# Moving weight tiles to other byte offsets, halving 512-column matmuls and turning query with value tiles in a fused HGRN2 and ConvFFN layer

## The chip, the cores and the metric

The kernel runs on one core of one Trainium2 chip. The metric is the device time of one execution in microseconds (us); the time of a kernel is the median of several executions. Five engines of the core work beside each other: PE (TensorE, the matmuls), DVE (VectorE), ACT (ScalarE), POOL (GpSimd) and SP (SyncE, which here issues the transfers).

## The reference

One layer over 256 latent and 256 context tokens with a model width of 2048: a bidirectional gated recurrence as token mixer, then a gated MLP with a width-3 convolution, each between two RMS norms with adaLN shift, scale and gate.

```python
q, f_fw, f_bw, v, g = jnp.split(h @ w_in, 5, axis=-1)          # w_in: 2048 x 10240
...
f = lb + (1 - lb) * jax.nn.sigmoid(f_raw)
dirs.append((heads(1 - f), heads(jnp.log(f))))
...
S = exp(b_end) * S + einsum('bhsk,bhsv->bhkv', kc * exp(b_end - b), vc)   # chunked scan, both directions
...
o = rms_norm(o, o_gain) ; y = (o * jax.nn.silu(g)) @ w_out     # 2048 x 2048
x_lat = x_lat + gt_ml * rms_norm(y, norm_mix_post)
...
gate, up = jnp.split(h @ ffn_w_in, 2, axis=-1)                 # 2048 x 11264
f = (silu(dwconv_centred(gate, conv_w, conv_b)) * up) @ ffn_w_out   # 5632 x 2048
x_lat = x_lat + gt_fl * rms_norm(f, norm_ffn_post)
```

Only the latent tokens leave the layer, so queries and gates are made for 256 tokens, and forget gates and values for all 512.

## The kernel before, in words

All large products are made in three float32r matmuls. `split` turns each float32 operand into a part `hi`, which ACT rounds to float32r, and the rest `lo`, which DVE subtracts; `mm3` (lines 197 to 202) then adds hi·hi, hi·lo and lo·hi into one PSUM bank. A matmul has a stationary operand, loaded into the array, and a moving operand that streams through it, one column after the other; the trace has a weight load (PEld) for each matmul.

A weight tile is 512 KB. The class `Stream` holds the list of all 452 weight tiles in the order of their use: `load` issues the DMA into one of four `w_raw` buffers, `prep` makes `w_hi` and `w_lo` (three buffers each, 4096 bytes per partition) a little ahead of the matmuls, and `next` hands a tile out. The order of the tiles is thus written by hand, in the calls of `ws.add`; the engines' own order follows from the code and the priorities in it, by a scheduler.

The stages in order of time are these.

- The start (to about 240 us): for each of eight pairs of row blocks the tokens are normed and modulated, and the first 512 columns of q, g, v and both forget gates are accumulated in SBUF (`start_latents`, `start_v`, `start_f`).
- The mixer's projections (240 to 890 us): for the head pairs p = 2 to 7, forget gates of both directions (`proj_ws` with 512 moving columns, tokens moving, weights stationary), queries (`one_bank`, `proj_ws` with 256 columns), values (`proj_xs`, weights moving, tokens stationary) and gates (`one_bank` again). After each tile `step` moves the generator `mixer` on, so that the scans of earlier head pairs (`scan`: strips of 32 columns, decays on DVE, copies on ACT, the readout `o`) lie between the projections' matmuls. `scan(p)` begins when the queries of p are there, and waits inside for v and g.
- The mixer's output product (890 to 985 us): `out_product` with z stationary and `w_out` moving, 512 columns; the rest of the last scan runs beside it (`mixed`, two steps for each weight tile).
- The norm between (985 to 1013 us).
- The MLP's first product (1013 to 1490 us): `ffn_w_in` stationary, h2 moving, 256 columns, with convolution and activation beside it.
- The MLP's output product (1490 us to the end): `out_product` with the activations `ah` and `al` stationary and `ffn_w_out` moving, 512 columns.

Where tiles lie in SBUF is set by their size and by tiles that hold nothing (`spacer`). Before the change the weights' parts start at 64 bytes modulo 256 in their partition, and the operands that meet them at 0:

```python
    SHIFT = 64
    edge = ctx.enter_context(tc.tile_pool(name="edge", bufs=1, side="right"))
    spacer(edge, 224)
...
        spacer(wpool, SHIFT)
...
        spacer(h2, 256 - SHIFT)
...
        spacer(hold[0], SHIFT)
```

Of the kernel before, what the change touches and what calls it, by code (L numbers as in the profile page):

```python
# [8 lines left out]
F32 = mybir.dt.float32  # L9
# [8 lines left out]
P = 128  # L18
# [18 lines left out]
def tile_hgrn2_convffn_layer(  # L37
# [26 lines left out]
    SHIFT = 64  # L64
# [43 lines left out]

    class Stream:
# [6 lines left out]
        def add(self, src, a, n):  # L116
            self.specs.append((src, a, n))

        def load(self, n):
            while len(self.raw) < min(n, len(self.specs)):  # L120
                src, a, w = self.specs[len(self.raw)]
# [7 lines left out]
        def prep(self, pool=wpool):  # L129
            i = len(self.done)  # L130
            with tc.high_priority(offset=0 if i < n_start else 400):
                self.load(i + 1)
                _, a, w = self.specs[i]
# [3 lines left out]
                hi = pool.tile([P, a, w], F32R, name="w_hi")  # L137
                lo = pool.tile([P, a, w], F32R, name="w_lo")
# [30 lines left out]
    for j2 in range(8):  # L169
        for sec in "qgvfb":  # L170
            ws.add(w_in[j2 * 256:(j2 + 1) * 256, SEC[sec]:SEC[sec] + 512].rearrange("(a p) n -> p a n", p=P), 2, 512)
    n_start = len(ws.specs)
    for p in range(2, NP):
        for sec in "fbqvg":
            for k4 in range(4):
                ws.add(in_src(sec, p, k4), 4, 256)
# [5 lines left out]
    def add_out(w, chunks):  # L182
        for c0, n in chunks:
            rows = P * (1024 // n)
            for r in range(0, w.shape[0], rows):
                ws.add(w[r:r + rows, c0:c0 + n].rearrange("(a p) n -> p a n", p=P), rows // P, n)

    add_out(w_out, MIX_CHUNKS)

    ws.plain = range(len(ws.specs), len(ws.specs) + PLAIN)  # L190
    for i in range(NFF):
        for up in range(2):
            for k4 in range(4):
                col = up * DFF + i * 256
                ws.add(ffn_w_in[k4 * 512:(k4 + 1) * 512, col:col + 256].rearrange("(a p) n -> p a n", p=P), 4, 256)
    add_out(ffn_w_out, FFN_CHUNKS)
# [12 lines left out]
    colsC = const.tile([P, P], F32, name="colsC")  # L209
    colsD = const.tile([P, P], F32, name="colsD")  # L210
# [313 lines left out]
    with tc.manual_schedule():  # L524
# [6 lines left out]
        spacer(wpool, SHIFT)  # L531
# [66 lines left out]
    def proj_ws(banks, wt, k4, width, first, last):  # L598
        hi, lo = wt
        for k in range(4):  # L600
            kt = k4 * 4 + k
            for h in range(2):
# [3 lines left out]
                    first and k == 0 and (own or h == 0), last and k == 3 and (own or h == 1))  # L606
# [275 lines left out]
    for p in range(2, NP):  # L882
# [46 lines left out]
    def mixed():  # L929
# [17 lines left out]
        spacer(h2, 256 - SHIFT)  # L947
# [10 lines left out]
        spacer(hold[0], SHIFT)  # L958
# [195 lines left out]
```

## Time and profile before

| | us |
|---|---|
| median of three runs | 1751.97 |
| the three runs | 1737.32, 1751.97, 1755.46 |
| the profiled execution, its own time | 1740.89 |
| its span, first to last instruction | 1738.9 |
| PE busy in the span | 1691.3 (97%) |
| DVE, ACT busy | 1154.2 (66%), 772.5 (44%) |

The profile is one execution. A matmul's entry lasts longer than its place in the stream, because the next one starts while it still drains; what the stream pays for one matmul is the distance between starts. It can be read from a stretch without gaps: a row of the view of stretches counts every matmul that touches the stretch, so the distance is (length of the stretch + mean duration of one) / count.

### The profile page before, as it was taken

The numbers are of one execution on the slowest core, as the hardware profiler recorded it, in microseconds if no ns is written. First come the engines' busy times: TensorE is split into PE (matmuls) and PEld (weight loads), VectorE is DVE, ScalarE is ACT, GpSimd is POOL, SyncE is SP. The second block draws the span as 40 slices with busy tenths as digits, with TensorE's granted clock in tenths as the row PEclk, the third lists the DMA queues.
The fourth block names the chain that finished last, engine by engine and source line by source line (L and its number), as shares of the span: only waits on it lengthen the run. The fifth ranks groups of instructions, "written<-read, shape, count | busy, mean of one in ns | idle before, by whom it ended". The sixth has DMA issues, their size and how long they took to land.

```text
span 1738.9 us, 31985 instructions
## 1 busy us (share of the span) xinstructions
PE 1691.3 (97%) x12990; PEld 1504.6 (87%) x12990; DVE 1154.2 (66%) x1856; ACT 772.5 (44%) x1176; POOL 3.4 (0%) x13
## 2 busy tenths in 40 slices
PE   6999999899999999999999899999999999999998
PEld 4777888888989889898988799999999999888886
DVE  5777798865548875588565688766666666544444
ACT  4322264454545344443454544444444444443443
POOL 0000000000000000000000000000000000000000
PEclk9999999999999999999999999999999999999999
DMA  9897657633326863677348579766666666655654
GB/s 349 284 294 240 224 172 233 209 110 110 109 74 199 280 224 99 194 234 246 115 154 277 183 243 324 250 194 194 192 193 194 194 194 194 203 196 193 200 192 147
DMA packets 274646, 352.57 MB, mean 203 GB/s; under 512 B 12954, under 2 KB 197675, under 8 KB 273987
## 3 DMA queue, kind: packets, MB, share of 16 engines
q1 hardware_dynamic: 274499, 350.53, 62.5%
q8 instruction: 102, 1.67, 0.4%
q14 instruction: 45, 0.37, 0.1%
HBM read 348.37 MB, written 2.11 MB: 202 GB/s over the span
## 4 chain that ended last, share of the span: by engine, by line
PE 81%; DVE 8%; DMA 6%; issue 2%; ACT 1%; SPq 0%; DVEq 0%; ACTq 0%
PE pj L200 25%; PE pj L202 25%; PE pj L201 25%; DMA ada_w<-in_ada_w_dram 4%; DVE ada_acc L363 3%; DVE w_lo L107 2%; PE o L416 1%; ACT w_hi L106 1%; DVE k L692 1%; PE mi L804 1%; PE sc L732 1%; DMA w_raw<-in_hgrn_w_in_dram 1%; DMA aw<-in_ada_w_dram 1%; DMA hTh<-in_x_dram 0%; PE o L823 0%
## 5 line engine op out<-in xcount | busy, mean ns | idle before, releaser
L107 DVE TENSOR_TENSOR w_lo<-w_raw,w_hi 128x1024 fp32r<-128x1024 f32 x452 | 552.5, 1223 | 396.3 <-ACT w_hi L106 392.7
L106 ACT CAST w_hi<-w_raw 128x1024 fp32r<-128x1024 f32 x452 | 472.9, 1048 | 683.3 <-PE pj L201 367.9
L202 PE MATMUL pj<-h2h,w_lo 128*128 128x256 f32 x1376 | 381.0, 277 | 3.9 <-DVE w_lo L107 3.9
L200 PE MATMUL pj<-h2h,w_hi 128*128 128x256 f32 x1376 | 380.3, 276 | 0.0
L201 PE MATMUL pj<-h2l,w_hi 128*128 128x256 f32 x1376 | 380.0, 276 | 0.0
L200 PE MATMUL pj<-hTh,w_hi 128*128 128x256 f32 (+1 forms) x1040 | 353.2, 340 | 3.5 <-ACT w_hi L106 1.9
L202 PE MATMUL pj<-hTh,w_lo 128*128 128x256 f32 (+1 forms) x1040 | 348.0, 335 | 0.7 <-DVE w_lo L107 0.6
L201 PE MATMUL pj<-hTl,w_hi 128*128 128x256 f32 (+1 forms) x1040 | 348.2, 335 | 0.0
L202 PEld LDWEIGHTS pj<-h2h,w_lo 128*128 128x128 f32 x1376 | 258.4, 188 | 5.6 <-DVE w_lo L107 5.5
L200 PEld LDWEIGHTS pj<-h2h,w_hi 128*128 128x128 f32 x1376 | 258.3, 188 | 0.9 <-issue 0.8
L201 PEld LDWEIGHTS pj<-h2l,w_hi 128*128 128x128 f32 x1376 | 258.4, 188 | 0.0
L200 PEld LDWEIGHTS pj<-hTh,w_hi 128*128 128x128 f32 x1040 | 196.3, 189 | 33.7 <-issue 5.0
L202 PEld LDWEIGHTS pj<-hTh,w_lo 128*128 128x128 f32 x1040 | 196.3, 189 | 24.6 <-DVE w_lo L107 1.1
L201 PEld LDWEIGHTS pj<-hTl,w_hi 128*128 128x128 f32 x1040 | 196.7, 189 | 21.6 <-DVE hTl L107 0.2
L363 DVE SCALAR_TENSOR_TENSOR ada_acc<-ada_w,cst,ada_acc 128x512 f32<-128x512 f32 x240 | 179.7, 749 | 45.3 <-DMA ada_w<-in_ada_w_dram 42.2
L202 PE MATMUL pj<-w_hi,al 128*128 128x512 f32 x352 | 138.7, 394 | 0.0
L201 PE MATMUL pj<-w_lo,ah 128*128 128x512 f32 x352 | 138.0, 392 | 0.0
L200 PE MATMUL pj<-w_hi,hTh 128*128 128x256 f32 (+1 forms) x448 | 136.1, 304 | 0.6 <-DVE q L468 0.6
L200 PE MATMUL pj<-w_hi,ah 128*128 128x512 f32 x352 | 136.6, 388 | 0.0
L202 PE MATMUL pj<-w_hi,hTl 128*128 128x256 f32 (+1 forms) x448 | 134.0, 299 | 0.0
L201 PE MATMUL pj<-w_lo,hTh 128*128 128x256 f32 (+1 forms) x448 | 133.8, 299 | 0.0
L200 PEld LDWEIGHTS pj<-w_hi,hTh 128*128 128x128 f32 x448 | 85.9, 192 | 4.8 <-DVE stage L466 1.1
(226 smaller groups left out, 1792.1 us busy)
## 6 DMA issues: line engine op xcount, KB each, us to landing
w_raw<-in_ffn_w_in_dram SPq DMA_DIRECT2D x172, 512.0 KB, 3.9
w_raw<-in_hgrn_w_in_dram SPq DMA_DIRECT2D x160, 512.0 KB, 4.2
ada_w<-in_ada_w_dram SPq DMA_DIRECT2D x256, 256.0 KB, 4.0
w_raw<-in_ffn_w_out_dram SPq DMA_DIRECT2D x88, 512.0 KB, 3.6
aw<-in_ada_w_dram SPq DMA_DIRECT2D x64, 512.0 KB, 8.7
w_raw<-in_hgrn_w_out_dram SPq DMA_DIRECT2D x32, 512.0 KB, 4.2
hTh<-in_x_dram SPq DMA_DIRECT2D x2, 1024.0 KB, 4.9
hTh<-in_ctx_dram SPq DMA_DIRECT2D x2, 1024.0 KB, 10.3
```

What stands on the lines that cost most here:

```text
L106: S.copy(out=hi, in_=src)
L107: V.tensor_tensor(out=lo, in0=src, in1=hi.bitcast(F32), op=ALU.subtract)
L200: PE.matmul(out=o, lhsT=lh, rhs=rh, start=first, stop=False, skip_group_check=True)
L201: PE.matmul(out=o, lhsT=lh, rhs=rl, start=False, stop=False, skip_group_check=True)
L202: PE.matmul(out=o, lhsT=ll, rhs=rh, start=False, stop=last, skip_group_check=True)
L363: V.scalar_tensor_tensor(out=acc, in0=aw, scalar=cst[:, r, 0:1], in1=acc, op0=ALU.mult, op1=ALU.add)
L416: PE.matmul(out=strip[32 * a:32 * (a + 1), :], lhsT=cst[:, r4 * 4 + a, :], rhs=aws[r4][:, a].rearrange("p s n -> p (s n)"), start=(r4 == 0 ...
L692: V.tensor_tensor(out=half(t, i, m), in0=half(t, i, m), in1=half(by, 1 - i, m)[:, :, 0:1].to_broadcast([P, 256 // m, m]), op=ALU.mult)
L732: PE.matmul(out=o[32 * b:32 * b + 32, 32 * i:32 * i + 32], lhsT=flat(lhs[b % 2])[:, s0:s0 + 32], rhs=flat(rhs[b % 2])[:, t0:t0 + 32], star ...
L804: PE.matmul(out=sps[:, cs], lhsT=kT[:, d, h, ct], rhs=v[:, 2 + ct, h * P:(h + 1) * P], start=(ct == 0), stop=(ct == 1))
```

## The change

It has three parts.

- Placement. Each weight part gets a tile of 4096 + 128 bytes, and its data start at a chosen byte of it: 76 where the weights are stationary (q, g, f, b, `ffn_w_in`, and all tiles of the start), 64 where they move (v, `w_out`, `ffn_w_out`). Since 4224 is 16 x 256 + 128, the three buffers start at 0, 128 and 0 modulo 256 by turns, so stationary weights lie at 76 or 204 and moving ones at 64 or 192; a spacer of 128 bytes makes `w_hi` and `w_lo` of one tile equal modulo 256. The spacers of before go; h2 now lies at 128 modulo 256, the tokens, z and the MLP's activations stay at 0. `colsC` and `colsD` are cut to 96 columns, which gives 256 bytes of room.
- Halves. `mm3` can make a 512-column product as two of 256 columns, the three matmuls of the first half and then those of the second. The forget gates (in the start for whole tiles, and in `proj_ws` where each head has its own bank) and the MLP's output product use it.
- In turn. For p = 2 to 7 a query tile and a value tile now alternate, four of each, with one `step` of 1.5 for a pair instead of 0.5 after each query tile and 1.0 after each value tile. The queries of p are complete only when its values are.

```diff
-    SHIFT = 64
+    STATIONARY, MOVING = 76, 64
...
+    def placed(pool, a, w, name, place):
+
+        t = pool.tile([P, a * w + 32], F32R, name=name)
+        return t[:, place // 4:place // 4 + a * w].rearrange("p (a n) -> p a n", a=a)
...
-                hi = pool.tile([P, a, w], F32R, name="w_hi")
-                lo = pool.tile([P, a, w], F32R, name="w_lo")
+                hi = placed(pool, a, w, "w_hi", place)
+                if i == 0:
+
+                    spacer(wpool, 128)
+                lo = placed(pool, a, w, "w_lo", place)
                 split(hi, lo, self.raw[i])
...
-        for sec in "fbqvg":
+        for secs in ("f", "b", "qv", "g"):
             for k4 in range(4):
-                ws.add(in_src(sec, p, k4), 4, 256)
+                for sec in secs:
+                    ws.add(in_src(sec, p, k4), 4, 256, MOVING if sec == "v" else STATIONARY)
...
-    def mm3(o, lhs, rhs, first, last):
+    def mm3(o, lhs, rhs, first, last, halves=False):
         (lh, ll), (rh, rl) = lhs, rhs
+        if halves:
+
+            for s in (slice(0, 256), slice(256, 512)):
+                mm3(o[:, s], lhs, (rh[:, s], rl[:, s]), first and s.start == 0, last and s.start > 0)
+            return
...
-                mm3(o, (hi[:, a, cs], lo[:, a, cs]), (hTh[kt], hTl[kt]), a == 0, a == 1)
+                mm3(o, (hi[:, a, cs], lo[:, a, cs]), (hTh[kt], hTl[kt]), a == 0, a == 1, True)
...
-                    first and k == 0 and (own or h == 0), last and k == 3 and (own or h == 1))
+                    first and k == 0 and (own or h == 0), last and k == 3 and (own or h == 1), own)
...
         q = new_q("q")
-        gated(q, one_bank(p), QS)
-        have[p]["q"] = q
+        qb = bank(ps_pj, "pj")
         vb = [bank(ps_pj, "pj") for _ in range(2)]
         for k4 in range(4):
+            proj_ws([(qb[:, h * 256:(h + 1) * 256], False) for h in range(2)], ws.next(), k4, 256, k4 == 0, k4 == 3)
             proj_xs(vb, ws.next(), k4, k4 == 0, k4 == 3)
-            step(p, 1.0)
+            step(p, 1.5)
+        gated(q, qb, QS)
+        have[p]["q"] = q
...
-    out_product(FFN_CHUNKS, list(zip(a_hi, a_lo)), grow[5], yo, fp, ffn_eps, ffn_done, 3)
+    out_product(FFN_CHUNKS, list(zip(a_hi, a_lo)), grow[5], yo, fp, ffn_eps, ffn_done, 3, halves=True)
```

Before, on PE, in a forget-gate tile of the projections (`pj` is the PSUM bank of a head, `hTh` and `hTl` the tokens' parts):

```order
L200 MATMUL pj_7559<-hTh0_300,w_hi_7476 128x512
L201 MATMUL pj_7559<-hTl2_662,w_hi_7476 128x512
L202 MATMUL pj_7559<-hTh0_300,w_lo_7477 128x512
L200 MATMUL pj_7560<-hTh0_300,w_hi_7476 128x512
L201 MATMUL pj_7560<-hTl2_662,w_hi_7476 128x512
L202 MATMUL pj_7560<-hTh0_300,w_lo_7477 128x512
```

After the change, on PE, the same place with another head pair's tile:

```order
L216 MATMUL pj_8268<-hTh0_300,w_hi_8164 128x256
L217 MATMUL pj_8268<-hTl0_302,w_hi_8164 128x256
L218 MATMUL pj_8268<-hTh0_300,w_lo_8165 128x256
L216 MATMUL pj_8268<-hTh0_300,w_hi_8164 128x256
L217 MATMUL pj_8268<-hTl0_302,w_hi_8164 128x256
L218 MATMUL pj_8268<-hTh0_300,w_lo_8165 128x256
```

Each matmul of 512 columns has become two of 256, in the same bank, with a weight load of its own for each.

Before, on PE, where the mixer's output product begins (L788 and L789 turn the last scan's keys, L804 and L806 make its states, `ada_acc` holds the first z):

```order
L788 MATMUL mi_9880<-ident_82,k0_9321 128x128
L789 MATMUL mi_9880<-ident_82,k1_9326 128x128
L200 MATMUL pj_9925<-w_hi_9822,ada_acc_9893 128x512
L201 MATMUL pj_9925<-w_lo_9823,ada_acc_9893 128x512
L202 MATMUL pj_9925<-w_hi_9822,ada_acc_9894 128x512
L200 MATMUL pj_9926<-w_hi_9822,ada_acc_9893 128x512
L201 MATMUL pj_9926<-w_lo_9823,ada_acc_9893 128x512
L202 MATMUL pj_9926<-w_hi_9822,ada_acc_9894 128x512
L200 MATMUL pj_9925<-w_hi_9822,ada_acc_9893 128x512
L804 MATMUL mi_9935<-v_9731,kT_9336 128x128 x2
```

After the change, on PE, the last scan's turn of its keys (now L803), further on in that product:

```order
L216 MATMUL pj_11258<-w_hi_11456,zh4_11242 128x512
L217 MATMUL pj_11258<-w_lo_11457,zh4_11242 128x512
L218 MATMUL pj_11258<-w_hi_11456,zl4_11250 128x512
L803 MATMUL mi_11474<-ident_82,k0_11015 128x128
L836 MATMUL o_11542<-v_10979,scD_11104 128x128
L216 MATMUL pj_11257<-w_hi_11483,zh5_11243 128x512
L217 MATMUL pj_11257<-w_lo_11484,zh5_11243 128x512
L218 MATMUL pj_11257<-w_hi_11483,zl5_11251 128x512
```

The turn of the last keys stood ahead of the first matmul of the output product, and now stands behind those of the tiles z1 to z4.

## Rows read from the trace of the kernel before

**Rows 1.** The page's first part and the granted clock in 40 slices.

```profile
PE 1691.3 (97%) x12990; PEld 1504.6 (87%) x12990; DVE 1154.2 (66%) x1856; ACT 772.5 (44%) x1176; POOL 3.4 (0%) x13
...
PEclk9999999999999999999999999999999999999999
```

**Rows 2.** The chain that ended last, shares of the span by engine.

```profile
PE 81%; DVE 8%; DMA 6%; issue 2%; ACT 1%; SPq 0%; DVEq 0%; ACTq 0%
```

**Rows 3.** Stretches by stage: length; PE, PEld, DVE, ACT, POOL busy (count); clock, DMA.

```profile
0.00:60.00 60.00, 43.34 (x301) 32.70 (x302) 34.38 (x80) 23.89 (x39) 1.38 (x9) 0.97 0.92 314
60.00:240.00 180.00, 178.07 (x1047) 138.71 (x1046) 142.98 (x260) 56.73 (x69) 0.00 (x0) 1.00 0.79 254
240.00:890.00 650.00, 637.50 (x5888) 566.57 (x5887) 456.56 (x910) 304.17 (x585) 0.99 (x2) 0.99 0.54 171
890.00:985.00 95.00, 94.55 (x441) 77.97 (x439) 56.17 (x74) 51.26 (x83) 0.00 (x0) 1.00 0.68 228
985.00:1013.00 28.00, 23.38 (x126) 20.53 (x127) 23.00 (x48) 14.69 (x36) 0.00 (x0) 0.94 0.53 168
1013.00:1490.00 477.00, 473.07 (x4143) 470.33 (x4141) 323.44 (x381) 225.82 (x263) 1.00 (x2) 1.00 0.69 217
1490.00:1739.00 249.00, 241.41 (x1055) 197.77 (x1053) 117.71 (x108) 95.97 (x105) 0.00 (x0) 0.99 0.56 188
```

**Rows 4.** Groups of PE's instructions by form: count, busy us, mean ns of one.

```profile
L202 PE MATMUL pj<-h2h,w_lo 128*128 128x256 f32 x1376 | 381.0, 277 | 3.9 <-DVE w_lo L107 3.9
L200 PE MATMUL pj<-h2h,w_hi 128*128 128x256 f32 x1376 | 380.3, 276 | 0.0
...
L201 PE MATMUL pj<-hTl,w_hi 128*128 128x512 f32 x496 | 196.8, 397 | 0.0
...
L201 PE MATMUL pj<-hTl,w_hi 128*128 128x256 f32 x544 | 151.4, 279 | 0.0
...
L202 PE MATMUL pj<-w_hi,al 128*128 128x512 f32 x352 | 138.7, 394 | 0.0
L201 PE MATMUL pj<-w_lo,ah 128*128 128x512 f32 x352 | 138.0, 392 | 0.0
L200 PE MATMUL pj<-w_hi,ah 128*128 128x512 f32 x352 | 136.6, 388 | 0.0
...
L201 PE MATMUL pj<-w_lo,hTh 128*128 128x256 f32 x384 | 108.6, 283 | 0.0
```

**Rows 5.** Stretches without a gap on PE, columns as in rows 3.

```profile
1200.00:1480.00 280.00, 280.00 (x2470) 279.04 (x2469) 172.75 (x194) 133.75 (x155) 1.00 (x2) 1.00 0.63 193
1495.00:1725.00 230.00, 230.00 (x1006) 188.72 (x1005) 106.58 (x90) 91.76 (x96) 0.00 (x0) 1.00 0.57 190
822.00:838.00 16.00, 16.00 (x70) 12.82 (x69) 4.03 (x4) 2.37 (x4) 0.00 (x0) 1.00 0.35 105
630.00:641.00 11.00, 11.00 (x96) 11.00 (x95) 7.52 (x9) 6.88 (x8) 0.00 (x0) 1.00 0.68 204
...
733.00:743.50 10.50, 10.50 (x95) 10.50 (x94) 8.61 (x12) 6.75 (x8) 0.00 (x0) 1.00 0.86 282
...
1003.50:1012.50 9.00, 9.00 (x43) 7.93 (x42) 7.66 (x12) 1.77 (x4) 0.00 (x0) 1.00 0.44 139
```

**Rows 6.** The same groups as rows 4, from 630 to 641 us.

```profile
L202 PE MATMUL pj<-hTh,w_lo 128*128 128x256 f32 x32 | 9.0, 281 | 0.0
```

**Rows 7.** The same groups, from 733 to 743.5 us.

```profile
L202 PE MATMUL pj<-hTh,w_lo 128*128 128x256 f32 x31 | 8.6, 276 | 0.0
```

**Rows 8.** PE's longest waits, 240 to 990 us: total us, times, longest.

```profile
PE mi L844 <- ACT tmp L836: 7.6, 2, 5.2
PE sc L1024 <- DVE dg L1018: 2.2, 1, 2.2
```

**Rows 9.** The last scan's tail in order of time on ACT: start us, duration us.

```profile
884.34 0.74 ACT L776 COPY scD<-sc 64x256 f32<-64x256 f32 x2
...
903.15 1.14 ACT L836 ACTIVATE tmp<-o,rs 128x128 f32<-128x128 f32 x4 [0.28 <-DVE rs L81]
```

More of the change, by code (lines that the diff above doesn't have):

```diff
@@ L114, in __init__, with add @@
             self.plain, self.early = (), None
-        def add(self, src, a, n):
-            self.specs.append((src, a, n))
+        def add(self, src, a, n, place):
+            self.specs.append((src, a, n, place))
         def load(self, n):
             while len(self.raw) < min(n, len(self.specs)):
-                src, a, w = self.specs[len(self.raw)]
+                src, a, w, _ = self.specs[len(self.raw)]
                 if len(self.raw) in self.plain:
@@ L132, in prep @@
                 self.load(i + 1)
-                _, a, w = self.specs[i]
+                _, a, w, place = self.specs[i]
                 if i in self.plain:
@@ L170, in tile_hgrn2_convffn_layer, with add_out @@
         for sec in "qgvfb":
-            ws.add(w_in[j2 * 256:(j2 + 1) * 256, SEC[sec]:SEC[sec] + 512].rearrange("(a p) n -> p a n", p=P), 2, 512)
+            ws.add(w_in[j2 * 256:(j2 + 1) * 256, SEC[sec]:SEC[sec] + 512].rearrange("(a p) n -> p a n", p=P), 2, 512,
+                   STATIONARY)
     n_start = len(ws.specs)
     for p in range(2, NP):
-        for sec in "fbqvg":
+        for secs in ("f", "b", "qv", "g"):
             for k4 in range(4):
-                ws.add(in_src(sec, p, k4), 4, 256)
+                for sec in secs:
+                    ws.add(in_src(sec, p, k4), 4, 256, MOVING if sec == "v" else STATIONARY)
     MIX_CHUNKS = [(0, 512), (512, 512), (1024, 512), (1536, 512)]
     FFN_CHUNKS = [(0, 512), (512, 512), (1024, 512), (1536, 512)]
-    def add_out(w, chunks):
+    def add_out(w, chunks, place):
         for c0, n in chunks:
@@ L185, in add_out @@
             for r in range(0, w.shape[0], rows):
-                ws.add(w[r:r + rows, c0:c0 + n].rearrange("(a p) n -> p a n", p=P), rows // P, n)
-    add_out(w_out, MIX_CHUNKS)
+                ws.add(w[r:r + rows, c0:c0 + n].rearrange("(a p) n -> p a n", p=P), rows // P, n, place)
+    add_out(w_out, MIX_CHUNKS, MOVING)
     ws.plain = range(len(ws.specs), len(ws.specs) + PLAIN)
@@ L208, in tile_hgrn2_convffn_layer @@
     colsB = const.tile([P, P], F32, name="colsB")
-    colsC = const.tile([P, P], F32, name="colsC")
-    colsD = const.tile([P, P], F32, name="colsD")
+    colsC = const.tile([P, 96], F32, name="colsC")
+    colsD = const.tile([P, 96], F32, name="colsD")
     cst = const.tile([P, KT, 32], F32, name="cst")
@@ L530, in tile_hgrn2_convffn_layer @@
         ws.load(1)
-        spacer(wpool, SHIFT)
         aws0 = ada_load(0)
@@ L946, in mixed @@
         h2 = h_ctx.enter_context(tc.tile_pool(name="h2", bufs=1))
-        spacer(h2, 256 - SHIFT)
         for k in range(KT // 2):
@@ L957, in mixed @@
         hold.append(xin_ctx.enter_context(tc.tile_pool(name="hold", bufs=MORE)))
-        spacer(hold[0], SHIFT)
         for i in range(4):
@@ L965, in out_product @@
     def out_product(chunks, lhs, gate, ys, pool, eps, done, nheld, beside=iter(()), first=None,
-                    after=None):
+                    after=None, halves=False):
         ntile = 2 * len(lhs)
@@ L986, in tile_product @@
                         mm3(os[t], (lh[:, i % 2, ts], ll[:, i % 2, ts]), (hi[:, a], lo[:, a]),
-                            i == 0, i == ntile - 1)
+                            i == 0, i == ntile - 1, halves)
             held = nheld if last else 0
```

5 lines of the change are left out of this document (3 added, 2 removed).

## The prediction

> **What bounds the kernel now.** I read the page first, then the chain, then a table of stretches by stage. PE is busy 97% of the span, at a granted clock of 1.0 nearly throughout [rows 1], and the chain that ended last runs 81% through PE [rows 2]. By stage [rows 3] PE has no gap worth an edit: in the projections 637.5 of 650 us, in the MLP's products 473.1 of 477 and 241.4 of 249; DVE and ACT are at 70% and 47% there. The longest waits between 240 and 990 us are 7.6 and 2.2 us in all [rows 8]. So a change gains only by fewer or shorter places in PE's stream, and the question is what a place costs.
>
> For that I took stretches without a gap and worked out the distance between starts, (length + mean of one) / count [rows 5]. The MLP's first product has (280 + 0.276) / 2470 = 113.5 ns for 256 columns, its output product (230 + 0.391) / 1006 = 229.0 ns for 512, a forget-gate stretch (16 + 0.394) / 70 = 234.2 ns for 512. And two stretches of the same line, operands and form differ: 630 to 641 us has (11 + 0.281) / 96 = 117.5 ns, 733 to 743.5 us has (10.5 + 0.276) / 95 = 113.4. The mean durations show it too, 281 ns [rows 6] against 276 [rows 7]: duration less 163 ns is the distance. So 256 columns run in one of two rhythms, **close (113.4 ns) or wide (117.5 ns)**, and what sets it is not in the instruction. The rows by form [rows 4] then say who ran how: 276 to 277 ns in the MLP's first product is close all through, 279 and 283 in the projections are mixtures. A 512-column matmul costs more than two close ones (226.8) and less than two wide ones (235).
>
> All rows are of one execution: 1738.9 us of span, 1740.9 of its own time, 11.1 under the median of 1752.0. The three runs spread over 18.1 us. If the 4128 matmuls of the MLP's first product drew the wide rhythm instead, that would be 4128 x 4.1 = 17 us; it fits, but no row shows it.
>
> **The change part by part.**
>
> Halves in the forget gates: 3 x 496 = 1488 matmuls [rows 4]. By the stretch they cost 234.2 ns, by the group's mean 397 - 163 = 234. Two close ones save 7.4 ns, 11.0 us in all; I take 10, because a new rhythm needs a few matmuls to settle at each tile. Two wide ones cost 0.8 ns more, +1.2 us. The close end is nearer: operands placed alike (weights stationary, tokens moving, 256 columns) average 279 ns, three above the close 276 and only two under the wide 281, yet part of that excess is the lowered clock (0.97 and 0.99 in the first and third stage of rows 3), and 4128 of the same pattern in the MLP were close. The extra weight loads, one for each new matmul, lie beside the stream as PEld does now (470 of 477 us there, [rows 3]).
>
> Halves in the MLP's output product: 3 x 352 = 1056 matmuls at 229.0 ns [rows 4, 5]. Close halves save 2.2 ns, 2.3 us; wide ones cost 6 ns, +6.3 us. I take -2. The nearest row is the value tiles, the only 256-column products with weights moving, and their 283 ns [rows 4] lean to wide; that end stays in the range.
>
> [...]
>
> Placement: the weights' part under a stationary load moves from 64 to 76 or 204 bytes modulo 256 with the tokens at 0, in the MLP to 76 or 204 with h2 at 128. Every offset between two operands that the trace holds is a multiple of 64 bytes, so no row prices 76. Bounds: in the good direction, the plain float32 matmuls at 1003.5 to 1012.5 us take 9 / 43 to 9.4 / 43, or 209 to 218 ns, for 256 columns [rows 5]; if a float32r column took just half of a plain one, 256 would take 109 ns, my estimate of the best that could be. In the bad direction the wide rhythm, 117.5. Between them I take the close rhythm everywhere, because it is the nearest row: most 256-column matmuls already have it. That is worth the present excess of the mixtures, (279 - 276) x 1632 + (283 - 276) x 1152 = 13 us, of which I give half to the two halvings of the clock that the projections hold and count -6. ACT and DVE write the parts at the new bytes; their 1.0 and 1.2 us for each tile lie under 2.7 us of matmuls or more, so even a quarter more there stays hidden.
>
> In turn: a pair of a query and a value tile holds 72 matmuls or 8.2 us, with two tiles' splits beside it, and nothing waits now; 0 for that. What costs is the end. The queries of p = 7 come four value tiles later, so the last scan, of which only the tail ran beside the output product, now has its last levels there, with PE in order behind them. In the trace its tail from the copy at 884.3 to the scaled output at 903.2 + 1.1 took 20 us [rows 9] with 48 gate matmuls (5.4 us) and some 36 of 512 columns under it; by the program's order there are now about 40 of 512 columns, 9 us, and some 4 us of small matmuls. So 0 (all covered) to 7 us are exposed; the waits for the same scaled copy, two with 7.6 us in all [rows 8], say that such a chain can show. I take +3.
>
> Sum on the profiled execution: 1740.9 - 10 - 2 - 6 + 3 = **1726 us**, 1.5% under the median. About 1% is what a measurement of this kernel can tell from no change.
>
> **The rivals.**
>
> Below the close rhythm. If the offset of 12 bytes beside the 64 keeps the weight load out of the stream's way, the 4128 + 1632 + 2 x 1488 = 8736 matmuls with placed stationary weights come to 109 ns: 8736 x 4.4 = 38 us less, 1688. [...] Against it: the fastest stretch of all is at 113.4 [rows 5].
>
> Placement does nothing. The two rhythms have the same offsets modulo 256, so what picks the rhythm may be the moment at which a stretch begins. Then part of the new halves are wide, the halves give perhaps -4, the 6 us stay, the tail costs 3, and the MLP's first product may draw either rhythm: 1740 to 1757, say 1745, no change. [...]
>
> Slower. The wide rhythm becomes the rule: 76 is the first offset here that is no multiple of 64, and a weight load that begins off it may disturb the stream for longer. All 12,000 matmuls of 256 columns (8736, 1152 values, 2112 halves) at 117.5 cost 12,000 x 4.1 = 49 us over my sum: 1775, 1.3% over the median. It is slower by more than 1% (over 1769.5) from 43.5 / 49 = 89% of them on. For it: both new parts rest on a rhythm of which the value tiles show more wide than close. Against it: the 3264 pieces with moving weights, a quarter, keep their offsets modulo 128. [...]
>
> **How the numbers follow.** Forecast 0.36, below the close rhythm 0.18, placement without effect 0.26, wide rule 0.20. Faster by over 1% are the first two less the upper edge of the forecast (over 1734.5) and with the lower edge of the third, 0.53; within 1% most of the third and that edge, 0.27; slower 0.20. For 8 in 10 the range must take in the fastest case at 1688 with 2 us below it and the wide rule up to 1772, where nearly all pieces are wide: 1686 to 1772.
>
> **What would show it.** In the new profile the groups by form should have mean durations near 276 ns for h2h, hTh and the value tiles; forget gates and MLP output should appear with 256 columns and about 276; below 273 the first rival holds, at 281 the third. The MLP's first product should take 475 us or less from its first to its last matmul, the output product about 240. PE's waits should have the last scan's copies and turns with 3 us, and none at a query or value tile. I am wrong if durations outside 272 to 281 turn up, or if a wait for `w_lo` or the scan's chain costs more than 7 us.

## The result and the profile after

The changed kernel takes **1754.9 us** (median of 20 executions, 1750.8 to 1760.0); the kernel before, run beside it, 1743.8 (20 executions, 1737.2 to 1756.4). The ratio is 1.0052 with an interval of 1.0033 to 1.0072: half a per cent longer, where 1.5% less was forecast. The ratios leave out single executions more than 1.5% above the fastest of their kernel, of which the ranges of the table below hold one each in "MLP halves", "after less placement" and "both halves, old places". The profiled execution has a span of 1756.8 us against 1738.9 and took 1758.6. Of these two, the one of before lies 2.9 us under its median and the one after 3.7 over it, so stages compared between them show 17.9 us where the medians show 11.1.

The page of the changed kernel, busy time by engine and the chain by engine, answers to [rows 1, 2]:

```profile
PE 1702.6 (97%) x15534; PEld 1628.8 (93%) x15534; DVE 1153.0 (66%) x1856; ACT 773.1 (44%) x1176; POOL 3.4 (0%) x13
...
PE 55%; DMA 4%; DVE 3%; issue 1%; ACT 1%; SPq 0%; DVEq 0%; ACTq 0%
```

PE has 2544 more matmuls, as the halves must give, and is busy 11 us longer; it remains the bound. The chain was followed back only part of the way here (its shares add up to 64%, before to 98%), so its shares don't compare with those of [rows 2]. By stage (columns as in [rows 3]; the last row is a stretch without a gap):

```profile
240.00:893.00 653.00, 633.88 (x6922) 618.79 (x6921) 444.80 (x875) 295.69 (x564) 0.99 (x2) 0.99 0.54 171
893.00:1020.70 127.70, 123.12 (x684) 101.15 (x682) 87.57 (x152) 70.72 (x136) 0.00 (x0) 0.97 0.63 204
1020.70:1499.80 479.10, 474.45 (x4137) 473.07 (x4136) 322.54 (x379) 226.22 (x262) 1.00 (x2) 0.99 0.68 215
1499.80:1756.80 257.00, 249.04 (x2115) 248.83 (x2113) 118.06 (x109) 96.36 (x105) 0.00 (x0) 0.99 0.58 183
...
1520.00:1740.00 220.00, 220.00 (x1870) 220.00 (x1870) 99.73 (x84) 85.41 (x90) 0.00 (x0) 1.00 0.59 185
```

Two places stand out. The MLP's output, 249 us before, takes 257 without a gap: (220 + 0.280) / 1870 = 117.8 ns for 256 columns, the wide rhythm all through, 2 x 117.8 - 229.0 = 6.6 ns for each former matmul, 7.0 us for 1056. And in the projections PE is idle for 653 - 633.9 = 19 us, against 12.5 in the third row of [rows 3].

The groups by form (columns as in [rows 4]; 276 is the close rhythm, 281 the wide one):

```profile
L216 PE MATMUL pj<-hTh,w_hi 128*128 128x256 f32 x1536 | 436.2, 284 | 3.5 <-ACT w_hi L106 1.9 <-ACT hTh L106 1.6
L217 PE MATMUL pj<-hTl,w_hi 128*128 128x256 f32 x1536 | 428.9, 280 | 0.0
...
L218 PE MATMUL pj<-h2h,w_lo 128*128 128x256 f32 x1376 | 382.3, 278 | 4.6 <-DVE w_lo L107 4.6
...
L216 PE MATMUL pj<-w_hi,ah 128*128 128x256 f32 x704 | 197.3, 280 | 0.0
```

Where the idle time lies, PE's waits in the projections of p = 5 (565.7 to 678.2 us; total us, times, longest) tell. This stretch took 112.5 us where it had 105.9, and its waits are all for parts that DVE makes:

```profile
PE pj L218 <- DVE w_lo L107: 3.1, 1, 3.1
PE mi L735 <- DVE ctmp L726: 1.8, 1, 1.8
PE mi L803 <- DVE k L707: 1.7, 1, 1.7
PE sc L747 <- DVE scB L773: 0.5, 1, 0.5
```

The longest of them in order of time (start us, duration us; the wait stands in brackets), and then the stretches of the wait and of the 3.4 us after it and after that:

```profile
636.50 0.28 PE L217 MATMUL pj<-hTl,w_hi 128*128 128x256 f32 x1
639.87 0.39 PE L218 MATMUL pj<-hTh,w_lo 128*128 128x256 f32 x1 [3.10 <-DVE w_lo L107]
640.09 0.33 PE L216 MATMUL pj<-hTh,w_hi 128*128 128x256 f32 x1
```

```profile
636.40:639.80 3.40, 0.37 (x4) 0.17 (x2) 2.62 (x4) 0.79 (x1) 0.00 (x0) 1.00 0.02 7
640.00:643.40 3.40, 3.40 (x17) 3.40 (x18) 2.68 (x3) 0.00 (x0) 0.00 (x0) 0.53 0.67 193
643.60:647.00 3.40, 3.40 (x32) 3.40 (x31) 1.23 (x1) 1.05 (x1) 0.00 (x0) 1.00 0.78 258
```

A wait of 3.1 us is followed by 3.4 us at a granted clock of 0.53, which hold 17 matmuls where the 3.4 us behind them, at 1.00, hold 32: 15 / 32 of 3.4 us, or 1.6 us, so this wait cost about half as much again. Stage by stage, from the first matmul of one to that of the next, the span grew in the projections by 5.2 us (645.2 to 650.4), in the mixer's output and the norm by 5.1 (123.1 to 128.2), in the MLP's first product by 3.2 (476.1 to 479.3) and in its output by 7.5 (249.3 to 256.8); the start became 3.1 shorter. Together that is 17.9.

### The profile page after: what moved, and what is told of

It is laid out like the page before. It is cut to its first block, busy times and chain, and to the rows that moved or that the text cites. A ratio compares the mean times of both kernels' runs of the same rounds, so it can differ in the third digit from the quotient of the medians.

```text
span 1756.8 us, 37057 instructions
## 1 busy us (share of the span) xinstructions
PE 1702.6 (97%) x15534; PEld 1628.8 (93%) x15534; DVE 1153.0 (66%) x1856; ACT 773.1 (44%) x1176; POOL 3.4 (0%) x13
## 4 chain that ended last, share of the span: by engine, by line
PE 55%; DMA 4%; DVE 3%; issue 1%; ACT 1%; SPq 0%; DVEq 0%; ACTq 0%
PE pj L216 17%; PE pj L218 17%; PE pj L217 17%; DMA ada_w<-in_ada_w_dram 4%; DVE w_lo L107 1%; DVE ada_acc L379 1%; PE pj L1093 1%; PE sc L1040 1%; PE sc L747 0%; ACT w_hi L106 0%; PE mi L819 0%; DVE k L707 0%; PE mi L735 0%; ACT xin L1031 0%; DVE yo L1135 0%
## 5 line engine op out<-in xcount | busy, mean ns | idle before, releaser
L216 PE MATMUL pj<-hTh,w_hi 128*128 128x256 f32 x1536 | 436.2, 284 | 3.5 <-ACT w_hi L106 1.9
L218 PE MATMUL pj<-hTh,w_lo 128*128 128x256 f32 x1536 | 428.5, 279 | 4.3 <-DVE w_lo L107 4.2
L217 PE MATMUL pj<-hTl,w_hi 128*128 128x256 f32 x1536 | 428.9, 280 | 0.0
L216 PEld LDWEIGHTS pj<-hTh,w_hi 128*128 128x128 f32 x1536 | 290.5, 189 | 14.3 <-issue 5.9
L218 PEld LDWEIGHTS pj<-hTh,w_lo 128*128 128x128 f32 x1536 | 290.5, 189 | 5.3 <-DVE w_lo L107 5.1
L217 PEld LDWEIGHTS pj<-hTl,w_hi 128*128 128x128 f32 x1536 | 291.0, 189 | 0.5 <-DVE hTl L107 0.2
L216 PEld LDWEIGHTS pj<-h2h,w_hi 128*128 128x128 f32 x1376 | 260.5, 189 | 0.9 <-issue 0.8
L216 PE MATMUL pj<-w_hi,ah 128*128 128x256 f32 x704 | 197.3, 280 | 0.0
L218 PE MATMUL pj<-w_hi,al 128*128 128x256 f32 x704 | 197.0, 280 | 0.0
L217 PE MATMUL pj<-w_lo,ah 128*128 128x256 f32 x704 | 196.9, 280 | 0.0
L218 PEld LDWEIGHTS pj<-w_hi,al 128*128 128x128 f32 x704 | 133.2, 189 | 0.0
```

The lines of the kernel that those rows point to most:

```text
L217: PE.matmul(out=o, lhsT=lh, rhs=rl, start=False, stop=False, skip_group_check=True)
L218: PE.matmul(out=o, lhsT=ll, rhs=rh, start=False, stop=last, skip_group_check=True)
```

## The experiments

Each kernel was timed beside the kernel before on the same chip (medians of before: 1740.1 to 1743.8 us). "To MLP" is the time from the first matmul of the projections to the first of the MLP, the last two columns are the MLP's two products, all three in the one profiled execution of each kernel; "order" is queries and values in turn.

| kernel | median (range), us | ratio to before [95%] | to MLP | MLP in | MLP out |
|---|---|---|---|---|---|
| before | 1743.8 (1737.2–1756.4) | | 768.3 | 476.1 | 249.3 |
| after: all parts | 1754.9 (1750.8–1760.0) | 1.0052 [1.0033, 1.0072] | 778.6 | 479.3 | 256.8 |
| order | 1741.9 (1738.7–1756.1) | 1.0010 [0.9978, 1.0042] | 766.4 | 478.3 | 249.3 |
| forget halves | 1741.3 (1737.2–1748.4) | 0.9989 [0.9961, 1.0017] | 765.7 | 476.4 | 249.6 |
| MLP halves | 1738.0 (1733.5–1763.6) | 0.9986 [0.9953, 1.0019] | 769.3 | 483.2 | 247.2 |
| placement | 1741.6 (1738.5–1744.3) | 0.9985 [0.9956, 1.0013] | 764.9 | 480.9 | 250.7 |
| after less MLP halves | 1749.3 (1747.1–1752.0) | 1.0026 [0.9999, 1.0054] | 776.8 | 475.2 | 250.9 |
| after, one place for each part | 1762.2 (1758.2–1767.1) | 1.0112 [1.0076, 1.0149] | 771.8 | 484.0 | 256.8 |
| after less placement | 1746.5 (1741.7–1769.4) | 1.0024 [0.9990, 1.0058] | 772.8 | 480.2 | 247.4 |
| placement, MLP halves | 1749.4 (1743.3–1752.4) | 1.0035 [1.0011, 1.0058] | 767.9 | 479.6 | 256.5 |
| after less order | 1747.2 (1744.8–1751.3) | 1.0031 [1.0013, 1.0050] | 770.0 | 475.8 | 256.8 |
| placement, forget halves | 1740.3 (1736.4–1744.8) | 0.9987 [0.9971, 1.0004] | 768.0 | 475.5 | 250.9 |
| both halves, old places | 1739.4 (1733.4–1763.8) | 0.9983 [0.9963, 1.0004] | 766.0 | 477.6 | 247.4 |
| after, whole matmuls ahead | 1752.8 (1750.8–1755.8) | 1.0058 [1.0039, 1.0077] | 772.9 | 477.7 | 255.9 |
| after less order, MLP in at 64 | 1748.9 (1748.1–1749.2) | 1.0043 [1.0028, 1.0058] | 768.3 | 476.8 | 256.8 |
| after less order, h2 at 0 | 1744.7 (1741.8–1749.9) | 1.0018 [1.0002, 1.0034] | 766.9 | 478.2 | 253.8 |
| after less order, MLP out at 0 | 1753.3 (1750.9–1754.2) | 1.0066 [1.0051, 1.0081] | 769.6 | 476.4 | 260.5 |
| both halves, old places, h2 at 128 | 1760.3 (1750.1–1763.8) | 1.0096 [1.0065, 1.0127] | 768.3 | 481.3 | 256.8 |
| both halves, chosen places, 64 | 1739.1 (1735.9–1743.1) | 0.9973 [0.9950, 0.9996] | 770.0 | 478.3 | 247.4 |
| both halves, chosen places, 76 | 1741.9 (1738.5–1745.7) | 0.9992 [0.9970, 1.0015] | 771.5 | 477.0 | 247.4 |

**Each part alone.** The four edits, each made in the kernel before, are pieces of the change's diff:

```diff
# order
-        for sec in "fbqvg":
+        for secs in ("f", "b", "qv", "g"):
...
-            step(p, 1.0)
+            step(p, 1.5)
# forget halves
-                mm3(o, (hi[:, a, cs], lo[:, a, cs]), (hTh[kt], hTl[kt]), a == 0, a == 1)
+                mm3(o, (hi[:, a, cs], lo[:, a, cs]), (hTh[kt], hTl[kt]), a == 0, a == 1, True)
# MLP halves
-                            i == 0, i == ntile - 1)
+                            i == 0, i == ntile - 1, halves)
# placement
-    SHIFT = 64
+    STATIONARY, MOVING = 76, 64
```

> The kernel before with query and value tiles in turn alone. Theory A (order): the turn is what costs in the projections and at the start of the output product; the head pairs p = 5 and 6 (112.5 and 110.3 us in the changed kernel against 105.9 and 106.3) and the first output product (128.2 against 123.1) are longer here too, 5 to 15 us in all, with waits for w_lo and for the last scan. Theory B (places): the order costs nothing, the kernel stays within 3 us of the one before, and those lengths come from the rhythm of the matmuls.

> The kernel before with the forget gates in halves alone, all offsets as before. Theory A (halves at the old offsets run close): 8 to 10 us less, the forget gates' groups at a mean of 276 to 278 ns. Rival (a second weight load for each 512 columns costs as much as it saves): within 3 us, means of 280 or more.

> The kernel before with the MLP's output product in halves alone. Theory A (weights moving in 256 columns run wide whatever else is changed): 6 to 8 us more, the last stage 256 to 257 us against 249, means of 280 ns. Rival (the rhythm is drawn at the stage's start, and the changed kernel drew badly): a mean of 276 and 2 us less in this profile, or times that spread over two values.

> The changed kernel's placement alone: 512-column matmuls and the old order. Theory A (204 bytes are bad and 76 good for 256 columns with the tokens at 0): the query and gate tiles at 204 at 118 to 123 ns, those at 76 at 113; few of the matmuls are such, so 0 to 4 us more in the projections; the MLP's first product with h2 at 128 is close in every execution, so times spread less than before's 19 us. Rival (placement without effect): the two values of before, 1738 to 1744 and 1750 to 1756, appear here too.

None shows a cost by itself, though the order's interval reaches 1.0042. The order takes 6.9 us out of the projections (645.2 to 638.3) and adds 5.0 in the output product and the norm (123.1 to 128.1), most of it work that moved there: PE's waits in these two are 4.5 us, before 4.7. The forget halves ran mostly close, about 114 ns on average where half of a whole matmul took 117 before, but their projections are no shorter, 644.4 against 645.2, since waits for `w_lo` (3.8 us, before 0.6) and for the readout's `tmp`, which DVE makes (3.4, before 0.7), took their place. PE's waits for these two in the projections, of before and then of the kernel with forget halves (total us, times, longest):

```profile
PE o L823 <- DVE tmp L811: 0.7, 1, 0.7
PE pj L202 <- DVE w_lo L107: 0.6, 1, 0.6
...
PE o L827 <- DVE tmp L815: 3.4, 2, 2.5
PE pj L206 <- DVE w_lo L107: 3.2, 2, 1.7
...
PE pj L205 <- DVE w_lo L107: 0.6, 1, 0.6
```

The MLP halves ran close, 247.2 us. The four ratios multiply to 0.9970, or 5 us less than before; all together gave 1.0052, or 9 us more. So two or more parts disturb each other.

**Which parts disturb each other.**

```diff
# after less MLP halves
-    out_product(FFN_CHUNKS, list(zip(a_hi, a_lo)), grow[5], yo, fp, ffn_eps, ffn_done, 3, halves=True)
+    out_product(FFN_CHUNKS, list(zip(a_hi, a_lo)), grow[5], yo, fp, ffn_eps, ffn_done, 3)
# after, one place for each part: the three buffers in one tile
+                big[name] = [pool.tile([P, 3 * 1024 + 32], F32R, name=name, bufs=1), 0]
...
+            at = place // 4 + n * 1024
# after less placement, and placement with MLP halves: pieces of the change put together
```

> The changed kernel with whole matmuls of 512 columns again in the MLP's output product; all else as changed. Theory 'alternating places' (the third tile of a buffer ring in three stands 128 bytes further modulo 256, so that halves at 64 and 192 in turn run wide, 117.8 ns, and stationary parts at 204 run wider than those at 76): the stage of the MLP's output product falls from 256.8 to about 249 us, and the time by 7 to 8 us, to 1747. Theory 'order and halves together' (the waits of the queries' new order, met by the shorter forget gates, cost the 10 us): the time stays within 3 us of the changed kernel, 1752 to 1756, since the projections are untouched. Theory 'drawn rhythm' (a stage draws its rhythm anew in each program): 1745 to 1755, with another stage wide.

> The changed kernel with the three buffers of each part in one tile one after the other, so that every stationary part stands at 76 and every moving part at 64 modulo 256; nothing else changes. Alternating places: the MLP's output product runs at the close 113.4 ns and takes 247 us (10 less), and the projections' matmuls that had 204 run at 114 instead of 118 ns (1114 of them, 4 us less, and about 1 us in the first stage): 1755 - 15 = 1740 us. Order and halves together: the waits in the projections stay, and the time with them, 1750 to 1755. Drawn rhythm: somewhere from 1738 to 1756, with at least one of the MLP's two products wide at an unchanged place.

> The kernel before with the queries and values in turn, the forget gates in halves and the MLP's output product in halves, and all parts at 64 as before: the change without its placement. Alternating places: the three parts add up, and the MLP's output is close, 247 us: 1742.7 - 1 - 1.4 - 2 to -5 = 1735 to 1738 us. Order and halves together: 1750 to 1755, the same as the changed kernel. Drawn rhythm: 1735 to 1755.

> The kernel before with the new placement and the MLP's output product in halves; order and forget gates as before. Alternating places: the halves at 64 and 192 run wide, the stage takes 256 to 257 us, and the time is 1742 + 7.5 = 1749 to 1750 us. Order and halves together: the two parts cost nothing, as each alone: 1737 to 1742, with the stage at 247 to 250. Drawn rhythm: either, 1738 to 1755.

Without the MLP halves the time falls by 5.6 us between the medians and by 4.5 by the ratios, toward what "alternating places" has, if less than its 7 to 8; the kernel with one place for each part contradicts that theory flatly. With every moving part at 64 its output product is still wide. Its stretch from 1106 to 1230 us, and two later ones, read the same way:

```profile
1106.00:1230.00 124.00, 124.00 (x1035) 124.00 (x1035) 73.78 (x83) 55.95 (x65) 0.00 (x0) 1.00 0.61 189
1250.00:1480.00 230.00, 230.00 (x2031) 230.00 (x2031) 143.63 (x161) 110.40 (x129) 0.00 (x0) 1.00 0.63 195
1520.00:1740.00 220.00, 220.00 (x1870) 220.00 (x1869) 99.74 (x84) 85.06 (x91) 0.00 (x0) 1.00 0.60 185
```

The MLP's first product runs at 120.1 ns, then, after a pause near 1241 us, at 113.4; its output follows without a pause at 117.8. The rhythm is a state that this stream kept for 1035 matmuls, and then the other for 2031. The kernel with all parts but the placement shows a wide stretch of the first product at the old places too, which no row of before had:

```profile
1110.00:1230.00 120.00, 120.00 (x1022) 120.00 (x1021) 72.05 (x82) 55.65 (x65) 0.00 (x0) 1.00 0.62 192
1245.00:1480.00 235.00, 235.00 (x2076) 235.00 (x2075) 146.96 (x166) 112.72 (x131) 0.00 (x0) 1.00 0.63 193
```

And in the table the output's halves are at 247 in the two kernels with old places and at 256 to 257 in the three with new ones, whatever the order: one disturbance is placement with MLP halves, 9.4 us. The other is in "to MLP": 771.8 to 776.8 in the three kernels with the order and the forget halves, 766.4 and 765.7 where only one of them is there. "Drawn rhythm" holds for the first product, which takes 475 to 484 us after its pauses without a pattern in the parts, but not for the output, which repeats.

**The order with the forget halves, and other pairs.**

```diff
# after less order
-        for secs in ("f", "b", "qv", "g"):
+        for sec in "fbqvg":
# after, whole matmuls ahead: ci is the number of the column block, i of the row block
-                            i == 0, i == ntile - 1, halves)
+                            i == 0, i == ntile - 1, halves and i > ci)
# placement with forget halves, and both halves at old places: pieces of the change put together
```

> The changed kernel with the queries' four tiles ahead of the values' four again, as before; placement and both halvings stay. Theory 'order and forget halves together' (the shorter forget gates bring PE to the first scan steps of the pair in turn before DVE has their operands, which neither part does alone): the stretch of p = 5 falls from 112.5 to 103 to 107 us, p = 4 rises from 102.6 to 106, the mixer's output product falls from 128.2 to 123 to 124, the MLP's output stays wide at 256.5: 1755 - 6 + 3 - 4.5 = 1747 to 1748 us. Rival 'only the wide rhythm of the MLP's output costs' (the order is worth 0, as it was alone): 1754 to 1756.

> The kernel before with the new placement and the forget gates in halves; order and MLP output as before. If the halves' gain is given back to waits on DVE's parts, as at the old places: 1740 to 1742 us, with 2 us or more of waits for the weights' low part. If placement lets it stand (the third of the tiles at 204 shifts what is late): 1735 to 1738. In both the MLP's first product settles to 113.3 ns after each pause, 475 to 481 us, and no execution lies above 1750.

> The kernel before with the forget gates and the MLP's output in halves, all parts at 64, order as before. The two parts add: 1742.5 - 1.4 - 2 = 1738 to 1740 us where the MLP's first product holds the close rhythm, with the output stage at 247 us; 5 to 18 us more in executions in which a pause leaves that product wide. Rival 'any two parts together cost': 1745 to 1750 throughout.

> The changed kernel, but the first one, two, three and four row blocks of the MLP's four column blocks (6, 12, 18 and 24 matmuls) are whole matmuls of 512 columns, and halves follow. Theory 'the rhythm is a state that a stream keeps until something else passes through it': each column block draws anew, so some of the four run at 113.3 ns (61.8 us) and others at 117.8 (64.2), none between, and the stage takes 247 to 255 us. Rival 'the operands' places set the rhythm': all four are wide again, 256 to 257 us, and the time is the changed kernel's.

Without the order the changed kernel came to 1747.2 us, and "to MLP" to 770.0. Over all kernels, those with both have 771.8 to 778.6 (five, mean 774.6), those with the forget halves and the old order 765.7 to 771.5 (ten, mean 768.4), the order alone 766.4: in these profiles the pair costs about 6 us that neither costs alone. In the same batch the two kernels that differ by the order and by 0.9 us in the output stand 5.6 us apart. The three pairs of rows that differ by the order alone, with the forget halves in both, have ratios 0.0021, 0.0039 and 0.0041 apart. That the order costs less by itself rests on one ratio, 1.0010 with an interval up to 1.0042, and on one profile.

The stages show where the difference lies, in us, old order and then in turn:

| pair | projections | mixer's output and norm |
|---|---|---|
| before; order | 645.2, 638.3 | 123.1, 128.1 |
| after less order; after | 648.1, 650.4 | 121.9, 128.2 |
| both halves, old places; after less placement | 643.7, 644.8 | 122.2, 127.9 |
| placement, forget halves; after less MLP halves | 646.3, 650.1 | 121.8, 126.6 |

The work that the order moves arrives in the mixer's output in all four. It leaves the projections shorter only beside the old forget gates. Waits are but a part of that: from "after less order" to "after" PE's idle time in the projections rises by 1.8 us (17.3 to 19.1), while the excess of the distances over 113.3 ns grows by 1.9 us at the lowered clock and by 2.4 elsewhere.

The other two kernels are at 0.9987 and 0.9983, no worse than before. Of the whole matmuls ahead neither the theory (247 to 255 us) nor its rival (256 to 257) holds: the stage took 255.9 us; three column blocks stayed wide, the second changed between close and wide with the weight tiles.

**What makes the output wide.**

```diff
# after less order, MLP in at 64
-                ws.add(ffn_w_in[k4 * 512:(k4 + 1) * 512, col:col + 256].rearrange("(a p) n -> p a n", p=P), 4, 256,
-                       STATIONARY)
+                       MOVING)
# after less order, h2 at 0
         h2 = h_ctx.enter_context(tc.tile_pool(name="h2", bufs=1))
+        spacer(h2, 128)
# after less order, MLP out at 0
-    add_out(ffn_w_out, FFN_CHUNKS, MOVING)
+    add_out(ffn_w_out, FFN_CHUNKS, 0)
# both halves, old places, h2 at 128
-        spacer(h2, 256 - SHIFT)
+        spacer(h2, 256 - SHIFT - 128)
```

> As 'after_without_turn' (new placement, both halvings, old order), but the weights of the MLP's first product at 64 and 192 instead of 76 and 204; h2 stays at 128. Theory 'handed over' (the output's rhythm is set by the places in the stage before it, since PE goes from one to the other without a pause): the output product comes out at 113.3 ns and 247.3 us, the time near 1747 - 9.4 = 1738 us. Rival 'own places': it stays at 117.8 ns and 256.8 us, and the time at 1745 to 1749. The first product no longer settles after pauses and may be wide for a while: up to 6 us more.

> As 'after_without_turn', but h2 at 0 instead of 128 modulo 256, as before the change; the weights at 76 and 204 stay. Handed over: 113.3 ns and 247.3 us in the output product if h2 was it, the time near 1738. Own places: 256.8 us and 1745 to 1749.

> As 'after_without_turn', but the moving weights of the MLP's output at 0 and 128 instead of 64 and 192; the stage before is untouched. Handed over: the output product stays wide, 256.8 us, and the time at 1745 to 1749. Own places: it changes, to 113.3 ns and 247.3 us or to a third rhythm.

> As 'old_places_both_halves' (all parts at 64, both halvings, old order), but h2 at 128 instead of 0. Handed over, if h2's place does it: the output product turns wide, 256.8 us, and the time goes from 1739 to 1748. If the weights' place does it, or the output's own places: it stays at 247.4 us and 1736 to 1742.

The last of these is the plainest. Between it and "both halves, old places" h2 moves by 128 bytes, with the tiles that lie behind it (the convolution's, and a few that are used before h2), and the output product reads none of them. Stretches just before and after the handover, of the kernel with h2 at 0 and then of the one with h2 at 128:

```profile
1475.00:1487.00 12.00, 12.00 (x108) 12.00 (x108) 8.03 (x11) 7.19 (x10) 0.00 (x0) 1.00 0.64 196
...
1505.00:1725.00 220.00, 220.00 (x1944) 220.00 (x1943) 103.29 (x90) 87.85 (x95) 0.00 (x0) 1.00 0.60 187
```

```profile
1480.00:1492.00 12.00, 12.00 (x108) 12.00 (x108) 7.41 (x10) 7.71 (x10) 0.00 (x0) 1.00 0.56 179
...
1505.00:1725.00 220.00, 220.00 (x1871) 220.00 (x1870) 99.63 (x84) 85.53 (x90) 0.00 (x0) 1.00 0.61 189
```

Ahead of it both count 108 matmuls in 12 us, the close rhythm. Behind it the one goes on at (220 + 0.276) / 1944 = 113.3 ns, the other at 117.8 with the same operands at the same places modulo 256. So the state is handed over, as that theory says, and h2's place decides which; the first of the four, at 256.8 with h2 still at 128, agrees. Over the table it holds throughout: the eight kernels with the output in halves and h2 at 128 take 255.9 to 260.5 us there, the five with h2 at 0 and all moving parts at 64 take 247.2 to 247.4. The time of the last, 1760.3 us, lies 12 us above what was expected: three of its five executions took 1760 to 1764, and in the profiled one, of 1752.3, the MLP's first product was wide as well for 1260 matmuls, up to its pause near 1236 us. But the output's own places count as well: with h2 at 0 in the new placement the tiles at 64 were wide and those at 192 close (253.8 us; (220 + 0.279) / 1892 = 116.4 ns on average, where two thirds at 117.8 and a third at 113.3 give 116.3), and at 0 and 128, under h2 at 128, they ran at (220 + 0.28) / 1843 = 119.5 ns on average:

```profile
1505.00:1725.00 220.00, 220.00 (x1843) 220.00 (x1842) 98.15 (x83) 84.54 (x89) 0.00 (x0) 1.00 0.61 186
```

The weights of the MLP's first product at 64 and 192 show one more thing, stretches 1067 to 1075.5 and 1077 to 1085.5 us of the groups by form:

```profile
L215 PE MATMUL pj<-h2h,w_hi 128*128 128x256 f32 x25 | 7.0, 280 | 0.0
...
L215 PE MATMUL pj<-h2h,w_hi 128*128 128x256 f32 x26 | 7.2, 276 | 0.0
```

Between two tiles of different place a wide stream (280 ns) turned close (276) here, without a pause. With one place for all it stayed wide for 1022 and for 1035 matmuls (above). This is what the placement does for the first product: wherever its buffers alternate, at 76 and 204 or at 64 and 192, a wide stretch ended within some 90 matmuls.

**Places chosen from this.** The buffers of a part in one tile, so that each can be put; h2 at 0, the moving parts all at 64, only the stationary parts of the first product alternating (in the second kernel those of the projections and the start too, at 76 and 204; in the code an odd place marks a ring whose middle buffer stands 128 bytes further):

```diff
+            at = place // 4 + n * 1024 + (64 if n == 2 else 0) + (32 if n == 1 and place % 4 else 0)
...
-    STATIONARY, MOVING = 76, 64
+    STATIONARY, MOVING, TURNING = 64, 64, 65
# in the second kernel
+    STATIONARY, MOVING = 77, 64
```

> Old order, both halvings, h2 at 0, the three buffers of a part in one tile so that each stands where it is put: all at 64, only the middle buffer of the MLP's first product at 192. If alternating stationary places bring a wide stream back to close (as with 76 and 204, and with 64 and 192 under h2 at 128), the first product takes 475 to 477 us in every execution; the output halves, entered as with the old places, run at 113.3 ns and take 247.4 us: 1735 to 1738 us median, none above 1746. Rival 'the alternation also changes what is handed over': the output at 117.8, 256.8 us, 1745 to 1748.

> As 'h2_at_0' (new placement, both halvings, old order), with the moving parts of the MLP's output all at 64 instead of 64, 192, 64; the stationary parts alternate between 76 and 204 as there. If the 192 between them made the tiles at 64 wide: 113.3 ns all through, 247.4 us, 1738 us. If the 76 in the stage before did: 117.8 ns all through, 256.8 us, 1747.

Both outputs are close, 247.4 us; the rows of the first kernel, a wide start of the first product (1016 to 1024.5 us), its long stretch (1100 to 1230) and the output (1505 to 1725):

```profile
L223 PE MATMUL pj<-h2h,w_hi 128*128 128x256 f32 x24 | 6.7, 281 | 0.0
...
L223 PE MATMUL pj<-h2h,w_hi 128*128 128x256 f32 x383 | 105.9, 276 | 0.0
...
L223 PE MATMUL pj<-w_hi,ah 128*128 128x256 f32 x648 | 179.1, 276 | 0.0
```

So the 192 between them, not the 76 ahead of them, made the tiles at 64 wide in "h2 at 0". Both times miss their forecasts, by 1 and by 4 us, since their projections came out longer ("to MLP" 770.0 and 771.5) and the first product of the first took 478.3, not 475 to 477. The kernel with places at 64 takes 1739.1 us, 0.9973 of before [0.9950, 0.9996]: twelve executions lie between 1735.9 and 1743.1, where those of before reach 1754.5 beside it. It is the only one of 19 whose interval excludes no change on the better side, and only just, which chance could also give; the change's order and its place 76 are not in it.

## Why the prediction was wrong

- **MLP output in halves, counted at -2.** The step that failed is the choice of the close end. The wide end (+6.3) came true, +7.5 in the stage. The choice was right for the halves at the old places (-2.1 in the stage, -1.9 in those with h2 at 0 and 64); what turned it is the placement: h2 at 128 is enough by itself (256.8 with all else at the old places), and with h2 at 0 the 192 among the moving tiles still costs part of it (253.8). Both stood in the texts without a price.
- **Placement, counted at -6.** "The close rhythm everywhere" held for the MLP's first product between its pauses, which it earned by the alternation of 76 and 204, not by 76. In the projections the distances within a stream of the profiled execution average 114.3 ns for parts at 76 and 118.0 at 204, where the kernel with all parts but the placement averages 115.0. So the one buffer of three at 204 gave back more than the others won; no run puts these parts at 192, so whether the 128 bytes or the 12 make 204 dear stays open. The half set aside for the clock was sized by two lowered stretches, where the trace of before has three in the projections (13.7 us). Alone the placement is worth 0.15%, which its interval doesn't tell from nothing, though no execution lay above 1744.3.
- **Forget gates in halves, counted at -10.** The rhythm gave about two thirds of what was counted: over the projections the excess of the distances over 113.3 ns fell from 11.3 to 5.9 us with halves at the old places, and the start became 1.4 us shorter. What failed beyond that is that nothing was said of who is late next: DVE's 456 us of work there [rows 3] don't shrink with PE's matmuls (over the whole span 1153.0 us after, 1154.2 before), and PE came to wait for its parts (3.8 us for `w_lo` with forget halves, before 0.6). The few matmuls in which a rhythm settles, set aside there, stand in the trace of before: behind a tile of 512 columns, from 732.7 us on, the distances are 121, 116 and 114 ns, then 113.
- **In turn, counted at 0 and +3.** The tail was not exposed, so +3 should have been 0; and the 0 in the projections holds only beside the old forget gates. Together with the halves the order costs about 6 us: work leaves the projections and they are no shorter for it, in part for waits like those of p = 5 above (3.1 us the longest) and the granted clock of 0.53 behind it. That DVE is late because the shorter gates bring PE there sooner is argued from these waits; no run took DVE's load away.
- **The sum.** It added four terms as if independent. Measured alone they are worth -5 us; the two pairs add about 6 and 9.4, together +10, and +9 was measured by the ratio. The 1.5% also set a sum on a profiled execution of 1740.9 against a median of three; the median of 20 came to 1743.8, so 1726 was 1.0% below before.

The signs named ahead appeared: durations of 284 ns lie outside 272 to 281, and the waits for `w_lo` (3.9 + 2.4 in the projections and 4.6 in the MLP) exceed 7 us. The first could not have failed to appear, since the same group of before, the first matmul of three, had 285. Of the rivals, "placement does nothing" comes nearest: its thought that the moment at which a stretch begins picks the rhythm fits the pauses (120.1 ns ahead of one, 113.4 behind it, with one place for each part), its 1740 to 1757 contains the time, but it missed that places decide at a handover (113.3 or 117.8 ns by h2's 128 bytes) and that a wide stretch ended within some 90 matmuls where they alternate. "Wide becomes the rule" came true in one stage only. No stage ran below 113 ns for 256 columns; the 109 ns of the first rival rest on half the time of a plain float32 column, the author's estimate, which no run shows.

Two halves against a whole matmul: 2 x 113.3 = 226.6 ns against (220 + 0.39) / 963 = 228.9 for 512 columns in the output of before, and 2 x 117.8 = 235.6 in that of after. The halves are cheaper in the close rhythm and dearer in the wide one.

What stays open: what it is that one stage hands to the next while both show 113.3 ns, and why 64 with 192 between is wide where 64 alone is close. The rhythm at a handover can so far only be tried.

## What to carry to other kernels

Price edits in pairs where they share a resource. Here the forget halves left the projections no shorter (644.4 us, before 645.2), since PE came to wait for parts that DVE makes (`w_lo` 3.8 us, before 0.6; `tmp` 3.4, before 0.7), and the order, which took 6.9 us out of the projections alone, left them 1.1 to 3.8 us longer beside the halves. When an operand is moved, look at the stages that come after it too, not only at those that read it (h2's 128 bytes cost the stage behind it 9.4 us), and at each buffer of a ring by itself (114.3 ns at 76, 118.0 at 204). The wait of 3.1 us on PE cost about one and a half times its length, by the estimate above, with 3.4 us at a granted clock of 0.53 behind it; look for such a stretch behind a wait before counting it.

## What was not expected of the hardware

- 256-column float32r matmuls ran at 113.3, 117.8 or about 120 ns (120.1 with one place for each part) with the same instruction, and a stream kept its rhythm for 1022 to 2470 matmuls; it changed at a pause (120.1 to 113.4 ns near 1241 us) and between tiles at another place modulo 256 (durations of 280 to 276 ns).
- 128 bytes in the place of h2 cost the following stage 9.4 us, though that stage doesn't read it.
- Two close matmuls of 256 columns (226.6 ns) are cheaper than one of 512 at 228.9 ns, by 1%; two wide ones (235.6) dearer, by 3%.
